# Row normalisation: per-row tensor_scalar instead of a broadcast multiply, and two rows of each tile summed on ScalarE

## The chip, the cores and the metric

The kernel runs on one core of one Trainium2 chip. The metric is the device time of one execution in microseconds (us), as the median of several runs. The profile is of one such execution; its span runs from the first to the last instruction.

## The reference

```python
batch, seq, dim = 32, 512, 1024          # x is float32
sums = np.sum(np.abs(x), axis=-1, keepdims=True)
return (x / (sums + 1e-8)).astype(np.float32)
```

Each of the 16,384 rows of 1024 numbers is divided by the sum of its absolute values. Each element is read once and written once: 67.11 MB in, 67.11 MB out.

## The kernel before

The input is seen as 16,384 rows. A tile holds up to R = 12 rows in each of the 128 partitions, 48 KB per partition and 6.29 MB in all. The list `rows` gives the rows per partition of each of the 11 tiles: ten tiles of 12 rows, and a last one of 8. The function `piece` says which rows of the input belong to a tile: tiles 0, 1 and the last one share one block of 32 rows per partition, and the others have a block of 12 rows per partition each.

Four tile buffers (`BUFS = 4`) rotate. The loop over tiles does four things for each. First, the SP queue issues the load of the whole tile (L78). From the fifth tile on, this issue waits until the store of the tile that had the same buffer has landed. Second, VectorE sums absolute values of all rows of the tile in one `tensor_reduce` (L51), adds the epsilon (L58) and takes the reciprocal (L60), which leaves one factor per row and partition in `inv`. Third, the rows are scaled in place. VectorE multiplies the first `kv` rows in one `tensor_mul` (L61), whose second input is `inv` broadcast along the row, and ScalarE scales the remaining rows one at a time with an activation whose scale is the row's factor (L68). For tile 0, ScalarE takes five rows; for tiles 1 to 6 it takes one; for the last four tiles it takes none. Fourth, the ACT queue, which is ScalarE's own instruction stream, issues the store of the whole tile (L85). The store waits for all scales of the tile, and what stands behind it in ScalarE's stream waits with it.

The order is written by hand (`manual_schedule`), so that each engine runs its instructions in the order of the loop. GpSimd and TensorE do no work on the data.

Of the kernel before, what the change touches and what calls it, by code (L numbers as in the profile page):

```python
# [1 line left out]

# [4 lines left out]

FP32 = mybir.dt.float32
EPS = 1e-8


@with_exitstack
def kernel(
    ctx: ExitStack,
    tc: tile.TileContext,
    x: bass.AP,
    out: bass.AP,
):
    nc = tc.nc
    P = nc.NUM_PARTITIONS  # L20

    x_flat = x.flatten_outer_dims()
    out_flat = out.flatten_outer_dims()
    n, d = x_flat.shape

    R = 12
    BUFS = 4  # L30
    HEAD = 32
    per_partition = n // P
    assert n % P == 0 and (per_partition - HEAD) % R == 0
    rows = [R] * ((per_partition - HEAD) // R + 2) + [HEAD - 2 * R]

    def piece(flat, i):
        head = flat[: P * HEAD, :].rearrange("(p r) d -> p r d", p=P)
        if i < 2:
            return head[:, R * i : R * (i + 1), :]
        if i == len(rows) - 1:  # L40
            return head[:, 2 * R :, :]
        a = P * (HEAD + R * (i - 2))
        return flat[a : a + P * R, :].rearrange("(p r) d -> p r d", p=P)

    sbuf = ctx.enter_context(tc.tile_pool(name="sbuf", bufs=BUFS))
    stats = ctx.enter_context(tc.tile_pool(name="stats", bufs=4))

    def normalize(x_tile, r0, k, kv):

        s = stats.tile([P, R], FP32)  # L50
        nc.vector.tensor_reduce(  # L51
            out=s[:, :k],
            in_=x_tile[:, r0 : r0 + k, :],
            axis=mybir.AxisListType.X,
            op=mybir.AluOpType.add,
            apply_absolute_value=True,
        )
        nc.vector.tensor_scalar_add(out=s[:, :k], in0=s[:, :k], scalar1=EPS)  # L58
        inv = stats.tile([P, R], FP32)
        nc.vector.reciprocal(out=inv[:, :k], in_=s[:, :k])  # L60
        nc.vector.tensor_mul(  # L61
            out=x_tile[:, r0 : r0 + kv, :],
            in0=x_tile[:, r0 : r0 + kv, :],
            in1=inv[:, :kv].unsqueeze(2).to_broadcast([P, kv, d]),
        )
        for r in range(kv, k):
            row = x_tile[:, r0 + r, :]
            nc.scalar.activation(  # L68
                out=row,
                in_=row,  # L70
                func=mybir.ActivationFunctionType.Copy,
                scale=inv[:, r : r + 1],
            )

    with tc.manual_schedule():
        for i, k in enumerate(rows):
            x_tile = sbuf.tile([P, R, d], FP32)
            nc.sync.dma_start(out=x_tile[:, :k, :], in_=piece(x_flat, i))  # L78


            if i == 0:
                normalize(x_tile, 0, k, k - 5)
            else:
                normalize(x_tile, 0, k, k - 1 if i + BUFS < len(rows) else k)
            nc.scalar.dma_start(out=piece(out_flat, i), in_=x_tile[:, :k, :])  # L85


# [1 line left out]
_INS = ['x']  # L89
_OUTS = [((32, 512, 1024), 'float32')]  # L90


# [23 lines left out]
```

## Time and profile before

| what | value |
|---|---|
| median of 11 runs | 316.89 us (316.56 to 320.44) |
| the profiled execution | 316.59 us, of which the span is 315.0 us |
| VectorE (DVE) busy | 268.7 us |
| ScalarE (ACT) busy | 13.5 us |
| L51, sums, 11 instructions | 138.2 us |
| L61, multiplies, 11 instructions | 126.5 us |
| L68, ScalarE's scales, 11 instructions | 12.2 us |
| a 6.29 MB load, from issue to landing, median | 37.9 us |
| a 6.29 MB store, from issue to landing, median | 43.8 us |

In the profile, DVE is VectorE, ACT is ScalarE, and SPq and ACTq are the streams that issue loads and stores. A row of a group of instructions gives the line of the kernel, the engine, the operation, what it writes and reads, how often it ran, its busy time, the mean of one in nanoseconds, and the idle time just before it with what ended that. The line of DMA digits gives, for 40 equal slices of the span, the busy share of the 16 DMA engines in tenths. The rows of the windows give the stretch, its length, the busy time of VectorE, ScalarE and GpSimd with the number of instructions, the clock of TensorE, the DMA share and the GB/s; a DMA packet counts where it ends, so that a share in a short window can pass 1.

### The profile page before, as it was taken

The numbers are of one execution on the slowest core, as the hardware profiler recorded it, in microseconds if no ns is written. First come the engines' busy times: TensorE is split into PE (matmuls) and PEld (weight loads), VectorE is DVE, ScalarE is ACT, GpSimd is POOL, SyncE is SP. The second block draws the span as 40 slices with busy tenths as digits, with TensorE's granted clock in tenths as the row PEclk, the third lists the DMA queues.
The fourth block names the chain that finished last, engine by engine and source line by source line (L and its number), as shares of the span: only waits on it lengthen the run. The fifth ranks groups of instructions, "written<-read, shape, count | busy, mean of one in ns | idle before, by whom it ended". The sixth has DMA issues, their size and how long they took to land.

```text
span 315.0 us, 170 instructions
## 1 busy us (share of the span) xinstructions
DVE 268.7 (85%) x44; ACT 13.5 (4%) x12; POOL 0.2 (0%) x4
## 2 busy tenths in 40 slices
DVE  0079999999999999999995997899699969999910
ACT  0010601001000100100100010000000000000000
POOL 0000000000000000000000000000000000000000
DMA  8999999999999999999999999999999999999997
GB/s 331 468 400 443 456 318 481 400 424 474 400 437 462 400 437 462 400 449 449 400 481 418 400 493 406 400 493 406 400 499 400 406 441 422 470 397 493 400 408 325
DMA packets 3168, 134.22 MB, mean 426 GB/s; under 512 B 352, under 2 KB 352, under 8 KB 352
## 3 DMA queue, kind: packets, MB, share of 16 engines
q1 hardware_dynamic: 1584, 67.11, 49.8%
q10 hardware_dynamic: 1584, 67.11, 49.2%
HBM read 67.11 MB, written 67.11 MB: 426 GB/s over the span
## 4 chain that ended last, share of the span: by engine, by line
DVE 53%; DMA 33%; another core or an unknown queue 9%; issue 0%; SPq 0%; DVEq 0%; ACTq 0%
DVE s L51 27%; DVE x_tile L61 24%; DMA x_tile<-in_x_dram 17%; DMA out_dram<-x_tile 16%; DVE inv L60 1%; DVE s L58 0%; SPq L78 0%; DVEq L60 0%; ACTq L85 0%
## 5 line engine op out<-in xcount | busy, mean ns | idle before, releaser
L51 DVE TENSOR_REDUCE s<-x_tile 128x12 f32<-128x12288 f32 (+1 forms) x11 | 138.2, 12562 | 30.4 <-DMA x_tile<-in_x_dram 30.4
L61 DVE TENSOR_TENSOR x_tile<-x_tile,inv 128x11264 f32<-128x11264 f32 (+3 forms) x11 | 126.5, 11504 | 0.4
L68 ACT ACTIVATE x_tile<-x_tile,inv 128x1024 f32<-128x1024 f32 x11 | 12.2, 1142 | 152.8 <-DVE inv L60 152.8
L60 DVE RECIPROCAL inv<-s 128x12 f32<-128x12 f32 (+1 forms) x11 | 2.5, 225 | 0.9
L58 DVE TENSOR_SCALAR s<-s 128x12 f32<-128x12 f32 (+1 forms) x11 | 1.9, 173 | 0.4
L68 ACT ACT_TABLE_LOAD x1 | 1.3, 1283 | 17.8 <-DMA x_tile<-in_x_dram 17.8
L100 POOL MEMSET const-bfloat16-1.0<- 128x1 bf16 x1 | 0.1, 102 | 0.0
L100 POOL MEMSET const-uint8-127<- 128x1 uint8 x1 | 0.1, 102 | 0.0
L100 POOL MEMSET const-float32-0.0<- 128x1 f32 x1 | 0.1, 98 | 0.2 <-issue 0.2
L100 POOL MEMSET const-float32-1.0<- 128x1 f32 x1 | 0.1, 98 | 0.0
## 6 DMA issues: line engine op xcount, KB each, us to landing
x_tile<-in_x_dram SPq DMA_DIRECT2D x10, 6144.0 KB, 37.9
out_dram<-x_tile ACTq DMA_DIRECT2D x10, 6144.0 KB, 43.8
x_tile<-in_x_dram SPq DMA_DIRECT2D x1, 4096.0 KB, 33.0
out_dram<-x_tile ACTq DMA_DIRECT2D x1, 4096.0 KB, 13.2
```

The lines of the kernel that those rows point to most:

```text
L51: nc.vector.tensor_reduce(out=s[:, :k], in_=x_tile[:, r0 : r0 + k, :], axis=mybir.AxisListType.X, op=mybir.AluOpType.add, apply_absolute_v ...
L58: nc.vector.tensor_scalar_add(out=s[:, :k], in0=s[:, :k], scalar1=EPS)
L60: nc.vector.reciprocal(out=inv[:, :k], in_=s[:, :k])
L61: nc.vector.tensor_mul(out=x_tile[:, r0 : r0 + kv, :], in0=x_tile[:, r0 : r0 + kv, :], in1=inv[:, :kv].unsqueeze(2).to_broadcast([P, kv, d]),)
L68: nc.scalar.activation(out=row, in_=row, func=mybir.ActivationFunctionType.Copy, scale=inv[:, r : r + 1],)
L100: nc = _bacc.Bacc("TRN2", target_bir_lowering=False, num_devices=1)
```

## The change

The scale of a row moves to VectorE for all rows. In place of one `tensor_mul` over many rows it issues one `tensor_scalar_mul` per row, whose factor is a column of `inv`. ScalarE no longer scales. Instead, in each tile but the first, it sums the absolute values of the last `k // 6` rows (two of 12, one of the last tile's 8) with an `Abs` activation, which writes its elements to a scratch tile `junk` in PSUM and its sum to the row's column of `s`. VectorE's `tensor_reduce` covers the other rows. The pool for `s` and `inv` has a buffer count of 11 instead of 4. Loads, stores, tiles, buffers and their order stay as they were.

```diff
-    stats = ctx.enter_context(tc.tile_pool(name="stats", bufs=4))
+    stats = ctx.enter_context(tc.tile_pool(name="stats", bufs=len(rows)))
+    psum = ctx.enter_context(
+        tc.tile_pool(name="psum", bufs=1, space=bass.MemoryType.PSUM)
+    )
+    junk = psum.tile([P, d], FP32)

-    def normalize(x_tile, r0, k, kv):
+    def normalize(x_tile, k, ka):
         s = stats.tile([P, R], FP32)
         nc.vector.tensor_reduce(
-            out=s[:, :k],
-            in_=x_tile[:, r0 : r0 + k, :],
+            out=s[:, : k - ka],
+            in_=x_tile[:, : k - ka, :],
             axis=mybir.AxisListType.X,
             op=mybir.AluOpType.add,
             apply_absolute_value=True,
         )
+        for r in range(k - ka, k):
+            nc.scalar.activation(
+                out=junk[:, :],
+                in_=x_tile[:, r, :],
+                func=mybir.ActivationFunctionType.Abs,
+                accum_out=s[:, r : r + 1],
+            )
         nc.vector.tensor_scalar_add(out=s[:, :k], in0=s[:, :k], scalar1=EPS)
         inv = stats.tile([P, R], FP32)
         nc.vector.reciprocal(out=inv[:, :k], in_=s[:, :k])
-        nc.vector.tensor_mul(
-            out=x_tile[:, r0 : r0 + kv, :],
-            in0=x_tile[:, r0 : r0 + kv, :],
-            in1=inv[:, :kv].unsqueeze(2).to_broadcast([P, kv, d]),
-        )
-        for r in range(kv, k):
-            row = x_tile[:, r0 + r, :]
-            nc.scalar.activation(
-                out=row,
-                in_=row,
-                func=mybir.ActivationFunctionType.Copy,
-                scale=inv[:, r : r + 1],
-            )
+        for r in range(k):
+            row = x_tile[:, r, :]
+            nc.vector.tensor_scalar_mul(out=row, in0=row, scalar1=inv[:, r : r + 1])
...
-            if i == 0:
-                normalize(x_tile, 0, k, k - 5)
-            else:
-                normalize(x_tile, 0, k, k - 1 if i + BUFS < len(rows) else k)
+            normalize(x_tile, k, 0 if i == 0 else k // 6)
```

In the changed kernel the sums are L55 (VectorE) and L63 (ScalarE), the epsilon L69, the reciprocal L71, the row scales L74, the load L79 and the store L81.

## The prediction

> **What bounds the kernel now.** I began with the shares and the 40 slices of the page, because they tell whether an engine or the memory traffic fills the span.
>
> ```profile
> span 315.0 us, 170 instructions
> DVE 268.7 (85%) x44; ACT 13.5 (4%) x12; POOL 0.2 (0%) x4
> ...
> DMA  8999999999999999999999999999999999999997
> ...
> q1 hardware_dynamic: 1584, 67.11, 49.8%
> q10 hardware_dynamic: 1584, 67.11, 49.2%
> HBM read 67.11 MB, written 67.11 MB: 426 GB/s over the span
> ```
>
> VectorE at 85% looks like the bound, but the two queues, q1 (loads) and q10 (stores), hold the 16 DMA engines for 49.8 + 49.2 = 99.0% of the span, 311.9 us. By the windows, the first packets end after 1.5 us and the last ones just before 313.0 us: 311.5 us with no hole in them. The sustained rate is 134.22 MB / 311.5 us = 0.431 MB/us. A 12-row tile is 6.29 MB, so loading and storing it takes 2 x 6.29 / 0.431 = 29.2 us of DMA, while VectorE needs 25.3 us for it. From about 140 us VectorE waits for loads:
>
> ```profile
> DVE s L51 <- DMA x_tile<-in_x_dram: 30.4, 6, 17.7
> ```
>
> Of the 30.4 us, 17.7 are the first load; the other five are later tiles. Then the windows: does the traffic change when VectorE rests?
>
> ```profile
> 165.00:170.00 5.00, 1.42 (x2) 0.00 (x0) 0.00 (x0) 1.00 1.07 462
> 170.00:175.00 5.00, 5.00 (x1) 0.00 (x0) 0.00 (x0) 1.00 1.09 472
> ```
>
> It doesn't: 462 GB/s with VectorE 28% busy, 472 with it always busy (packets count where they end, so a 5 us window scatters around 431). Finally the end, where a chain must surface even under full traffic:
>
> ```profile
> 256.36 12.95 DVE L51 TENSOR_REDUCE s<-x_tile 128x12 f32<-128x12288 f32 x1 [2.52 <-DMA x_tile<-in_x_dram]
> ...
> 269.88 12.96 DVE L61 TENSOR_TENSOR x_tile<-x_tile,inv 128x12288 f32<-128x12288 f32 x1
> 282.76 8.68 DVE L51 TENSOR_REDUCE s<-x_tile 128x8 f32<-128x8192 f32 x1
> ...
> 291.99 8.69 DVE L61 TENSOR_TENSOR x_tile<-x_tile,inv 128x8192 f32<-128x8192 f32 x1
> ```
>
> VectorE ends at 300.7 and the last store (4.19 MB) is issued then and lands 13.2 us later. Its bytes alone take 4.19 / 0.431 = 9.7 us, so up to 313.0 - 9.7 = 303.3 us the DMA engines still drain the store of tile 9. The last store reaches its queue in time, with about 1 us to spare (a first packet ends 0.8 us after its issue at the start). The chain of waits gives VectorE 53% only because it follows this last hand-over backwards; the bound is DMA bytes, from 1.5 to 313.0 us.
>
> **What the Trainium skill says.** "DMA: Bandwidth & Descriptors", section "Queues, rings and completion order": an engine serves its queues round robin, a packet at a time. The trace agrees: from 60 to 250 us, q1 has 50.4% and q10 49.7%. The same page, "Where 436 GB/s comes from", gives a ceiling of 435 GB/s at the SBUF ports; the 434 GB/s of those 190 us sits on it. "SBUF — State Buffer", section "SBUF: two separate sides": computation and DMA have separate ports; the windows above agree. "VectorE: DVE Perf Modes", section "The perf-mode tier table": fp32 tensor_scalar on SBUF runs at two elements a cycle (1227 ns for 2048), tensor_tensor and tensor_reduce at one. The trace agrees on the last two (about 1.054 ns per element); it has no large tensor_scalar.
>
> **The change, part by part.** Fit first: the 7168-element multiply took 7.625 us and the 12288-element reduce 12.950, both 0.155 us plus 1.0417 ns per element.
>
> *Multiply to 12 row scales.* Removed: 11 tensor_tensor, 126.5 us. Added: 128 tensor_scalar of 1024 elements with a pointer scalar. At the skill's two elements a cycle each costs 0.155 + 0.533 = 0.69 us, 88 us in all. At one element a cycle it would be 0.155 + 1.067 = 1.22 us, 156 us in all. The low bound is 0.55 (the fixed part overlapped), the high one 1.31 (1.22 and a pointer fetch of 0.09, which is what "ScalarE: Activation LUTs", section "What ACT_TABLE_LOAD costs", gives for a pointer on ScalarE, an analogy). I take 0.69.
>
> *Two rows' sums to ScalarE.* The nine full tiles after the first reduce 10 rows, 10.82 us instead of 12.95; the last tile 7 rows, 7.62 instead of 8.68. Saved: 9 x 2.13 + 1.06 = 20.2 us of VectorE. ScalarE gets 19 Abs activations. The nearest row is L68, 1.14 us; with an accumulator somewhere between 1.04 and 2.3. Two take 2.1 to 4.6 us beside a 10.82 us reduce.
>
> *ScalarE's old scales* (11 activations, 12.2 us) go. Tile 0 loses a helper: its scale was 7.62 us beside five activations and becomes 12 x 0.69 = 8.3, or 14.7 at one a cycle; its store is issued at about 39.6 (or 45.9) instead of 38.9 us. The cover is the first four loads: 25.2 MB keep the engines fed to 1.5 + 58.4 = 59.9 us without a store. Cost nothing.
>
> *Waits.* VectorE's add at L69 now waits for the activations too; behind it stand the reciprocal and the scales, and behind those the store. On ScalarE's queue, store i waits for VectorE and holds the activations of tile i+1, which start when VectorE starts that tile's reduce. The worst is tile 1: store 0 issued at 39.6, its issue 0.35, table load 1.28, two activations 2.3: done at 43.5, while the reduce runs from 39.5 to 50.3. Cover 6.8 us; nothing is paid. The load of tile i+4 no longer waits for an activation; what comes last there is the store of tile i, as before. Stats buffers go from 4 to 11 and the junk tile sits in PSUM, which nothing else uses: nothing. The number, sizes and order of DMAs on the SP and ACT queues stay the same; POOL has none.
>
> *Sum.* VectorE: 268.7 - 126.5 + 88 - 20.2 = 210 us, 67% of the span. A full tile takes 10.82 + 0.51 + 8.3 = 19.6 us instead of 25.3, against 29.2 us of DMA. The tail: load 9 is gated by the store of tile 5, which advances at the DMA's pace, so it lands at about 256.4 as before, and load 10 at 280.5 (issued 247.5, 33.0 us to landing). VectorE ends tile 9 at 276.0 and tile 10 at 280.5 + 7.62 + 0.51 + 5.5 = 294.1; the last store is issued 6.6 us earlier and simply queues longer. What comes late next is nothing: the bytes are the same. Some 58 us off VectorE, and close to 0 off the span. A small gain is possible: from 295.0 to 313.0 us 7.34 MB moved in 18.0 us, where 0.431 MB/us takes 17.0, so up to 1 us may be lost in a ragged hand-over between the last two stores, which the earlier issue would smooth. I take 0.3.
>
> Against the profiled execution (315.0 span, 1.6 around it, 316.59) this gives 316.3; the median of the 11 runs stands 0.3 higher, at 316.89. Forecast **316.6**.
>
> **Rivals.**
> *A, the row scales are slow and VectorE becomes the bound (slower).* Let p be the price of a row. VectorE without waits: 31.2 (tile 0's scales start) + 8 x 11.33 + 11.33 + 8.13 + 128 p = 141.3 + 128 p; issue and a store that finds an empty queue (9.7 + 2.4 fixed, from load 0's 17.0 us for 14.6 us of bytes) and 1.1 to the span's end add 13.2. So 154.5 + 128 p, which passes 315.0 at p = 1.25 us; below it DMA hides everything, above it each 0.01 us costs 1.3 us. At 1.31 us the span is 322.2, the time 323.8. For it: no row of the page shows the fast mode, and many small instructions replace a long one. Against: the skill's price is 0.69, and even plain one-a-cycle (1.22) stays below the point. Chance 0.07; a further 0.04 for a DMA rate that drops by over 0.5% under VectorE's quicker accesses, about 319, which the windows speak against.
> *B, clearly faster.* For the faster case DMA must move more per us. At 434 GB/s throughout, 134.22 MB take 309.3 us; with 1.5 ahead and 2.0 behind, span 312.8, time 314.4. For it: in the first 60 us only 24.58 MB moved, 1.8 us less than at that rate. Against: that stretch keeps its four loads and its late first store. Chance 0.05.
> *C, the sums or scales don't overlap as said* (activations longer than the reduce): each would need over 5 us, against 1.14 in L68. Below 0.01, in A's share.
>
> **How the numbers follow.** A measurement here can tell about 0.5%, 1.6 us. No change 0.84, faster 0.05, slower 0.11. The likeliest case alone spans 315.8 (the whole ragged us gained) to 317.8 (the upper part of the 11 runs); reaching into A's low end and B's upper end: 315.4 to 318.6.
>
> **What would show it.** Right: DMA queues again near 99% and 426 GB/s; the row scales near 0.69 us; VectorE near 210 us; its waits for loads up from 30 to some 85 us; ScalarE about 23 us plus the table load; the last store issued some 6 us earlier and landing some 6 us later after issue, at the same 314 us. Wrong: a zero in the DMA slices, row scales above 1.25 us, an L69 wait on ScalarE, or DMA at 99% with packets that take longer.

## The result: 319.26 us, some 0.6% slower, and the profile after

The changed kernel takes 319.26 us (median of 13 runs, 318.55 to 320.77) where the kernel before takes 317.01 us (50 runs). The ratio is 1.0064, with a 95% interval of 1.0046 to 1.0081, so the change costs 1.5 to 2.6 us. The forecast was 316.6 us and no change, with a range up to 318.6. The runs of one kernel below, h2, lie in two groups (12 from 316.85 to 318.4 us, 10 from 319.27 to 321.37 us), so that its median of 318.31 stands between them.

The page's shares and groups first. Nearly everything that was said of the engines holds:

```profile
span 317.1 us, 305 instructions
DVE 207.9 (66%) x161; ACT 23.1 (7%) x39; POOL 0.2 (0%) x4
...
DMA  8999999999999999999999999999999999999994
...
q1 hardware_dynamic: 1584, 67.11, 49.5%
q10 hardware_dynamic: 1584, 67.11, 48.9%
q14 instruction: 2, 0.02, 0.0%
...
L55 DVE TENSOR_REDUCE s<-x_tile 128x10 f32<-128x10240 f32 (+2 forms) x11 | 117.9, 10721 | 84.8 <-DMA x_tile<-in_x_dram 84.8
L74 DVE TENSOR_SCALAR x_tile<-x_tile,inv 128x1024 f32<-128x1024 f32 x128 | 85.8, 747 | 0.4
L63 ACT ACTIVATE junk<-x_tile 128x1024 f32<-128x1024 f32 x19 | 19.5, 1027 | 219.6 <-DMA x_tile<-in_x_dram 203.5
```

VectorE's busy time fell to 207.9 us (210 were forecast), its wait for loads rose to 84.8 us (85 were forecast), and L69 never waits for ScalarE. The time that VectorE gave up became waiting, because the DMA engines still hold the bytes. Two things are new. The page lists a third DMA queue, q14, with two packets of 8 KB that it names instruction; below they are called fetches. And the last slice of DMA is a 4 where it was a 7: the end is drawn out.

The end in windows of 1 us (length, busy time of VectorE, ScalarE and GpSimd, clock, DMA share, GB/s), before and then after:

```profile
312.00:313.00 1.00, 0.00 (x0) 0.00 (x0) 0.00 (x0) 1.00 0.83 360
313.00:314.00 1.00, 0.00 (x0) 0.00 (x0) 0.00 (x0) 1.00 0.01 0
314.00:315.00 1.00, 0.00 (x0) 0.00 (x0) 0.00 (x0) 1.00 0.00 0
```

```profile
312.00:313.00 1.00, 0.00 (x0) 0.00 (x0) 0.00 (x0) 1.00 0.84 360
313.00:314.00 1.00, 0.00 (x0) 0.00 (x0) 0.00 (x0) 1.00 0.08 33
314.00:315.00 1.00, 0.00 (x0) 0.00 (x0) 0.00 (x0) 1.00 0.08 33
```

From 312 to 313 us the two are the same. After it, 0.08 of 16 engines' time is about 1.2 us of one engine, and 33 GB/s for 1 us is one packet of 32 KB: in each of these microseconds a single packet of the last store starts. (A window counts a packet where it starts, not where it ends, as the text ahead of the prediction and the prediction have it: this store lands at 316.13 us, and the windows from 315 us on are empty. No step of the argument rests on the difference.) In the changed kernel **one** DMA engine is still working when the other fifteen are done. The trace has the time at which each engine's share of a transfer landed. For the last store, 15 shares landed by 313.79 us before and by 313.97 after; the sixteenth at 313.88 before and at 316.13 after. The last engine was 0.1 us behind and is now 2.2 us behind; the span grew by 2.1 us. (The profiled executions differ by 2.62 us, 319.21 to 316.59: the other 0.5 us lie around the span, and no run here explains them.)

This lag has a history. It is at most 0.2 us until 80 us. The first fetch starts at 96.33 us and takes 0.31 us (1.0% of 16 engines' time in the window from 96 to 98 us):

```profile
q14 instruction: 1, 0.01, 1.0%
```

The load packet behind it takes 2.35 us where 48 KB normally take 1.815. The next landing, at 103 us, shows a lag of 0.86 us, about the sum of the two delays (0.31 + 0.53). At 256 us it is 1.4 us, at 281 us 2.2. Read packet by packet from 46 us on, the trace of before has 0.04 us of delay beyond the usual 1.815 and 1.213 us (48 and 32 KB), that of after 3.2 us, over 19 packets. The trace doesn't name a packet's engine, but the packets of one engine follow each other almost without a gap, so that they can be strung into 16 chains of 88 load and 88 store packets each. The chain that fetched at 96.33 us is the one that ends last, and 2.2 of the 3.2 us, in 10 of the 19 packets, are its own. The second fetch, at 285.22 us, is on another engine and left the lag as it was.

### The profile page after: what moved, and what is told of

The parts are those of the page before. It is cut to its first block, busy times and chain, and to the rows that moved or that the text cites. A ratio compares the mean times of both kernels' runs of the same rounds, so it can differ in the third digit from the quotient of the medians.

```text
span 317.1 us, 305 instructions
## 1 busy us (share of the span) xinstructions
DVE 207.9 (66%) x161; ACT 23.1 (7%) x39; POOL 0.2 (0%) x4
## 4 chain that ended last, share of the span: by engine, by line
another core or an unknown queue 45%; DMA 30%; DVE 17%; SPq 1%; DVEq 0%; issue 0%
DMA x_tile<-in_x_dram 15%; DMA out_dram<-x_tile 14%; DVE s L55 10%; DVE x_tile L74 7%; SPq L79 1%; DVE inv L71 0%; DVEq L107 0%; DVE s L69 0%; DVEq L69 0%
## 5 line engine op out<-in xcount | busy, mean ns | idle before, releaser
L55 DVE TENSOR_REDUCE s<-x_tile 128x10 f32<-128x10240 f32 (+2 forms) x11 | 117.9, 10721 | 84.8 <-DMA x_tile<-in_x_dram 84.8
L74 DVE TENSOR_SCALAR x_tile<-x_tile,inv 128x1024 f32<-128x1024 f32 x128 | 85.8, 747 | 0.4
L63 ACT ACTIVATE junk<-x_tile 128x1024 f32<-128x1024 f32 x19 | 19.5, 1027 | 219.6 <-DMA x_tile<-in_x_dram 203.5
L63 ACT ACT_TABLE_LOAD x1 | 1.3, 1283 | 39.7 <-DVE x_tile L74 39.7
L63 ACT ACTIVATION_READ_ACCUMULATOR junk<-x_tile 128x1 f32 x19 | 3.5, 186 | 0.0
L71 DVE RECIPROCAL inv<-s 128x12 f32<-128x12 f32 (+1 forms) x11 | 2.5, 226 | 0.4
L69 DVE TENSOR_SCALAR s<-s 128x12 f32<-128x12 f32 (+1 forms) x11 | 1.9, 173 | 1.1
```

Of the source, the lines that this page charges most:

```text
L55: nc.vector.tensor_reduce(out=s[:, : k - ka], in_=x_tile[:, : k - ka, :], axis=mybir.AxisListType.X, op=mybir.AluOpType.add, apply_absolut ...
L63: nc.scalar.activation(out=junk[:, :], in_=x_tile[:, r, :], func=mybir.ActivationFunctionType.Abs, accum_out=s[:, r : r + 1],)
L74: nc.vector.tensor_scalar_mul(out=row, in0=row, scalar1=inv[:, r : r + 1])
```

## The experiments

Three questions: which part of the change makes one engine late; does an instruction fetch alone do it; and why do the same fetches cost 2 us in one kernel and little in another? Each ratio is to the kernel before, run again beside it (its medians went from 316.82 to 317.25 us).

**e1, the sums alone.**

```diff
-        for r in range(k):
-            nc.vector.tensor_scalar_mul(out=row, in0=row, scalar1=inv[:, r : r + 1])
+        nc.vector.tensor_mul(out=x_tile[:, :k, :], in0=x_tile[:, :k, :],
+                             in1=inv[:, :k].unsqueeze(2).to_broadcast([P, k, d]))
```

> One part alone: ScalarE sums two rows of each tile but the first, as in the changed kernel, and VectorE scales each tile with one broadcast multiply as the kernel before. VectorE keeps 44 instructions. Theory I (long instruction streams are fetched in 8 KB pieces through one of the 16 DMA engines, which then runs late to the end): no fetch inside the span, the last packets of all 16 engines end within 0.5 us of each other near 313.5 us, time 316.6 to 317.2. Theory II (the row scales on VectorE slow some transfers through the memory ports): also 316.6 to 317.2. Theory III (ScalarE's sums or their scratch tile do it): about 319.2.

Measured: 324.05 us, ratio 1.0217 (1.0189 to 1.0244). All theories missed. The edit also left VectorE alone with tile 0's multiply (12.96 us in place of 7.62), so the first store was issued at 44.21 us. Windows of this kernel:

```profile
60.00:90.00 30.00, 29.82 (x5) 2.30 (x4) 0.00 (x0) 1.00 1.01 398
90.00:120.00 30.00, 29.82 (x6) 4.60 (x8) 0.00 (x0) 1.00 1.01 437
```

From 60 to 90 us the DMA engines are as busy as later (1.01) but move 398 GB/s instead of 437: packets on all engines take longer, and the engines stay busy. f1 below tests whether the late store did it.

**e2, the row scales alone.**

```diff
-            normalize(x_tile, k, 0 if i == 0 else k // 6)
+            normalize(x_tile, k, 0)
```

> The other part alone: VectorE sums all rows and scales them with one tensor_scalar per row, ScalarE only issues stores. VectorE has 161 instructions. Theories I and II: about 319.2, with packets of queue 14 inside the span under theory I. Theory III: 316.6 to 317.2.

Measured: 318.48 us, ratio 1.0049 (1.0029 to 1.0068), one fetch at 80 us, last engine 2.2 us behind, and it is the engine that fetched. ScalarE's sums are not needed for most of the loss, so theory III falls.

**e3, the kernel before with 132 small memsets on idle GpSimd.**

```diff
...
+            for _ in range(12):
+                nc.gpsimd.memset(pad[:, :], 0.0)
             x_tile = sbuf.tile([P, R, d], FP32)
```

> The kernel before with 132 memsets of one number per partition added on GpSimd, which nothing else waits for. VectorE and ScalarE are as before. Theory I, if any engine's instruction stream is fetched that way: a queue 14 packet early in the span (GpSimd runs its memsets in the first 20 us), one engine late by 0.8 us or more to the end, time 317.5 to 319.3. Theory I, if only VectorE's long stream counts, and theories II and III: 316.6 to 317.2.

Measured: 320.35 us, ratio 1.0101 (1.0083 to 1.0119), a fetch at 11.7 us, last engine 3.1 us behind, again the one that fetched. No instruction of VectorE or ScalarE was changed, and no data moved. Here instructions on an idle engine, which nobody waits for, cost 1%.

**e4, e1 with 117 small memsets on VectorE.**

```diff
...
+            for _ in range(k - 1):
+                nc.vector.memset(pad[:, :], 0.0)
             nc.scalar.dma_start(out=piece(out_flat, i), in_=x_tile[:, :k, :])
```

> The kernel of the sums alone, with k - 1 memsets of one number per partition added on VectorE after each tile's multiply (117 in all), so that VectorE has 161 instructions as in the changed kernel but no row scale. Theory I: queue 14 packets at about 100 and 285 us, one engine late by some 2 us at the end, about 319.2. Theories II and III (II: no row scales, so no harm): 316.6 to 317.2 for II, 319.2 for III only if the sums alone give it as well.

Measured: 324.1 us, ratio 1.0221 (1.0202 to 1.0241), as e1 and outside all ranges: with its first store at 44.12 us, what the fetches add can't be told from what the late store costs. Repeated as f2.

**f1, the sums alone, tile 0 as before.** Edit: in e1, `kv = k - 5` for tile 0, whose other five rows ScalarE scales.

> The sums on ScalarE alone again, but with tile 0 scaled as in the kernel before (seven rows on VectorE beside five on ScalarE), so that the first store is issued at 38.9 us and not at 44. Theory I (8 KB instruction fetches set one DMA engine back): the streams are short, a fetch comes after 285 us at the earliest, time 316.8 to 317.8. If ScalarE's sums themselves cost the time seen in e1_sums_only: 322 to 324. If the late first store did: back to 317.

Measured: 317.36 us, ratio 1.0002 (0.9981 to 1.0022). Its first store is issued at 38.80 us, and between 60 and 90 us it moves

```profile
60.00:90.00 30.00, 29.82 (x6) 4.54 (x8) 0.00 (x0) 1.00 1.01 437
```

So the sums cost nothing that can be told from noise, and a first store that is 5.4 us later cost e1 6.7 us, with slower packets on all engines. Why those packets are slow was not settled. The fetches came at 260.6 and 292.8 us, the first of them earlier than expected.

**f2, f1 with 117 memsets on VectorE.**

```diff
...
+            for c in range(R * i, R * i + k - 1):
+                nc.vector.memset(pad[:, c : c + 1], 0.0)
             nc.scalar.dma_start(out=piece(out_flat, i), in_=x_tile[:, :k, :])
```

> The kernel of f1_sums_tile0 with 117 memsets of one number per partition added on VectorE (k - 1 after each tile's multiply, each to its own column, without waits): VectorE has 161 instructions as in the changed kernel, but no row scale. Theory I: queue 14 packets near 100 and 285 us, the last landing about 2 us behind that of the other engines, 1.5 to 2.5 us over f1_sums_tile0. Theory II (the row scales' own memory accesses do it): the same as f1_sums_tile0 within 0.5 us.

Measured: 317.61 us, ratio 1.0014 (0.9998 to 1.0030). The fetches came at 105.4 us, with VectorE's added instructions, and at 261.6, where f1 has one too. The first delayed its engine by 0.31 + 0.54 us, as in the changed kernel. But at the end the last engine was 0.5 us behind, not 2. The fetch is there and the loss is not. By the ranges set down, this speaks for theory II, which g1 below tests; if theory I is to stand, something must make the lag grow in the changed kernel and not here.

**f3, the pad of e3 late** (a copy that depends on tile 9's reciprocal, then 131 memsets on GpSimd).

> The kernel before with a copy of one number and 131 memsets on GpSimd that begin when tile 9's reciprocal is done (about 270 us), where e3_pool_pad had its 132 at the start. If a fetch costs what it takes from its engine once: one 0.3 to 0.8 us delay whenever it comes, and e3's 3.5 us came from something else in its early fetch. If the delay grows from tile to tile once one engine is out of step: late is cheap, 317.0 to 317.9; at e3's 320.3 if only the number of instructions counts.

Measured: 317.21 us, ratio 0.9999 (0.9978 to 1.0019), fetch at 295.0 us, last engine 0.2 us behind. The number of instructions alone costs nothing that can be told from noise.

**f4, 44 memsets in place of e3's 132.**

> e3_pool_pad with four memsets per tile in place of twelve, 44 in all, so that GpSimd's stream ends before the point at which e3's was fetched (after 78 of its recorded instructions). If the fetch is the cause: no queue 14 packet inside the span, 316.6 to 317.2. If GpSimd's instructions cost by their number: a third of e3's 3.5 us, about 318.0.

Measured: 317.64 us, ratio 1.0010 (0.9988 to 1.0032), no fetch inside the span, last engine 0.3 us behind. The median lies above the first range and below the second. The interval holds no change, and excludes e3's 1% and just excludes the third of it (0.37%).

Comparing the traces gave a second half for theory I. Each DMA engine alternates between a load packet and a store packet. In the kernel before, whose first store is issued at 38.91 us, the engines take their first store packet at two times: 4 of 16 at 43.4 to 43.9 us, the other 12 one packet later, at 45.3 to 45.9. From there on they work in **two groups**, half a cycle of one load and one store packet apart. In the changed kernel the first store comes 0.34 us later, no engine catches the earlier place, and all 16 alternate **in one step** (45.3 to 45.7 us). From the timelines, before and after:

```profile
38.91 0.38 ACTq L85 DMA_DIRECT2D out_dram<-x_tile  x1
```

```profile
39.25 0.37 ACTq L81 DMA_DIRECT2D out_dram<-x_tile  x1
```

The 0.34 us come from tile 0: twelve row scales on VectorE (8.04 us) in place of seven rows there (7.62) beside five on ScalarE.

**g1, the changed kernel with tile 0 as before.**

```diff
+        if ka == 0:
+            kv = 0
+            nc.vector.tensor_mul(...)          # rows 0 to 6
+            for r in range(k - 5, k): nc.scalar.activation(...)
+        for r in range(kv):
```

> The changed kernel with tile 0 alone scaled as in the kernel before (seven rows on VectorE beside five on ScalarE); tiles 1 to 10 keep their row scales and ScalarE's sums. The first store is issued at about 38.9 us instead of 39.25. Theory I with its second half (a fetch costs 0.3 to 0.9 us where the engines alternate between load and store packets in two groups, as behind a first store at 38.9 us, and grows to 2 us or more where 15 of them keep one step, as behind one at 39.3): 317.2 to 318.0. Theory II (the row scales' own accesses do it): 319.2, as the changed kernel.

Measured: 317.32 us, ratio 1.0023 (1.0003 to 1.0042). First store at 38.93 us, fetches at 127.1 and 261.9 us, last engine 0.2 us behind. 116 row scales are left and the loss is nearly gone, so theory II falls.

**g2, g3 and g4** were to set step and fetch one by one on the kernel before (their expectations follow in this order): g2 with a memset of 230 numbers on VectorE ahead of tile 0's multiply, g3 with that and a GpSimd pad from tile 2 on, g4 with the pad alone.

> The kernel before with one memset of 230 numbers per partition (0.4 us) on VectorE between the reciprocal and the multiply of tile 0, so that the first store is issued at about 39.3 us as in the changed kernel; no other instruction is added, and no instruction fetch falls inside the span. If the time of the first store alone costs: 318.5 to 319.5. If it needs a fetch as well: 316.7 to 317.4, with all engines ending together.

> g2_store0_later with a copy of one number and 131 memsets on GpSimd that begin at tile 2's reciprocal (about 78 us), so that one 8 KB fetch falls near 100 us, about where the changed kernel had its first. Theory I with its second half: one engine late by some 2 us at the end, 318.3 to 319.5. If the fetch costs the same whatever the step of the engines: as g4_fetch_only.

> The same GpSimd instructions as in g3_later_and_fetch on the kernel before, without the memset in tile 0: first store at 38.9 us, one fetch near 100 us. Theory I with its second half: one engine late by 0.5 to 0.9 us, 317.2 to 318.0. If the step of the engines doesn't matter: as g3_later_and_fetch.

Measured: g2 317.0 us (ratio 0.9983, 0.9960 to 1.0007), g3 317.27 (1.0014, 0.9987 to 1.0041), g4 317.38 (1.0007, 0.9991 to 1.0023). The memset overlapped with its neighbours and moved nothing: the first store of g2 and g3 was issued at 38.89 us and their engines ran in two groups. So all three are of the two-group kind, and they show that a fetch near 100 us (g3, g4) costs at most 0.41% there, the upper end of the wider interval. The other half needed a longer memset.

**h1, g2 with 500 numbers.**

> The kernel before with a memset of 500 numbers per partition on VectorE ahead of tile 0's multiply (230 moved the first store by nothing in g2_store0_later, since the memset overlapped). The first store should now be issued at 39.2 to 39.4 us, as in the changed kernel. No fetch inside the span. Theory I with its second half (in-step engines alone cost nothing, a fetch is needed): 316.7 to 317.4, with the first store packets of all 16 engines between 45.4 and 46.1 us. Rival (a first store at 39.3 costs by itself): 318.5 to 319.5.

Measured: 317.67 us, ratio 1.0036 (1.0005 to 1.0067). The time lies between the two ranges, and the interval just excludes no change. First store at 39.16 us, all 16 engines in one step, no fetch inside the span, and in the profiled execution (316.95 us) all land together (15th 313.86, last 313.88). Its runs spread, though: nine up to 318.05, five from 319.21 to 321.0. What those five lost isn't in the trace, so it isn't excluded that one step costs time without a fetch in some executions.

**h2, h1 with the fetch.**

> h1_store0_39_3 with g3's copy and 131 memsets on GpSimd from tile 2's reciprocal on: one fetch near 100 us. Theory I with its second half: the engine that fetches falls back from tile to tile, last landing 1.5 to 3 us behind, 318.3 to 320. Rival (a fetch costs its 0.3 to 0.9 us whatever the step): 317.0 to 317.8.

Measured: median 318.31 us, ratio 1.0045 (1.0016 to 1.0073), the two groups of runs named above. The profiled one took 319.29 us: first store at 39.34 us, one step, fetch at 101.5 us, and the last engine falls from 0.5 us behind at 139 us to 1.1 at 256 and 2.2 at the end. Its last windows repeat those of the changed kernel:

```profile
313.00:314.00 1.00, 0.00 (x0) 0.00 (x0) 0.00 (x0) 1.00 0.08 33
314.00:315.00 1.00, 0.00 (x0) 0.00 (x0) 0.00 (x0) 1.00 0.08 33
```

The median just reaches theory I's range, but the trace speaks against the theory. The engine that fetched lost 0.31 + 0.21 us and ended with the others. The engine that ended 2.2 us late fetched nothing inside the span: its first store packet began at 46.0 us, 0.4 us after the last of the other fifteen, it was 0.6 us behind at 52 us, and ten slow packets, 2.2 us in all, followed from 82 us on. So an engine that is late for another reason falls back in the same way; the fetch is one way to make it late, and not a necessary one. Nor do the times tell h1 and h2 apart: 5 of 14 runs lie above 319.2 us without the fetch, 10 of 22 with it, and the two intervals nearly coincide.

**h3, the changed kernel with one row of tile 0 on ScalarE.**

```diff
-        for r in range(k):
+        kv = k - 1 if ka == 0 else k
+        for r in range(kv):
...
+        for r in range(kv, k):
+            nc.scalar.activation(out=row, in_=row, func=..., scale=inv[:, r : r + 1])
```

> The changed kernel with one row of tile 0 scaled on ScalarE beside VectorE's eleven, so that the first store is issued some 0.6 us earlier, near 38.6 us; the other 127 row scales and ScalarE's sums stay. Theory I with its second half: the engines split into two groups and the fetches cost little, 317.0 to 318.0. Rival (the number of instructions, or the row scales of tiles 1 to 10): 318.8 to 319.4.

Measured: 317.70 us (317.27 to 318.24), ratio 1.0019 (1.0001 to 1.0038). One row of 128 moved; 127 row scales, 19 sums and both fetches (98.2 and 281.9 us) stayed. No run reaches the changed kernel's lowest, 318.55 us. From its timeline and its last windows:

```profile
38.77 0.37 ACTq L90 DMA_DIRECT2D out_dram<-x_tile  x1
```

```profile
313.00:314.00 1.00, 0.00 (x0) 0.00 (x0) 0.00 (x0) 1.00 0.01 0
314.00:315.00 1.00, 0.00 (x0) 0.00 (x0) 0.00 (x0) 1.00 0.00 0
```

The tail is gone. The engine that fetched at 98.2 us lost 0.31 + 0.54 us, as in the changed kernel, and had no further slow packet. (h3 also brings ScalarE's table load forward, from 39.7 to 17.9 us. That isn't the cause: e2 has no activation at all and shows the lag all the same.) All traces but those of e1 and e4, whose first store comes at 44 us:

| kernel | first store issued, us | engines in the early place | fetch before 130 us | last engine behind the 15th, us | last landing, us |
|---|---|---|---|---|---|
| before, g2, f4, f3, f1 | 38.80 to 38.91 | 4 to 14 | none | 0.1 to 0.3 | 313.9 to 314.8 |
| f2, g1, g3, g4, h3 | 38.74 to 38.93 | 6 to 10 | one | 0.1 to 0.5 | 313.9 to 314.6 |
| h1 | 39.16 | 0 | none | 0.0 | 313.9 |
| changed, e2 | 39.25, 39.30 | 0 | one, on the last engine | 2.2 | 316.1, 315.9 |
| h2 | 39.34 | 0 | one, on another engine | 2.2 | 316.2 |
| e3 | 39.30 | 1 | one, at 11.7, on the last engine | 3.1 | 316.8 |

All four kernels that leave an engine over 2 us late have their engines in one step (15 of 16 in e3), and none of the ten with two groups does, although five of these have an early fetch. So the step, which the time of the first store sets, divides them. In one step an engine that is late falls further back: in the changed kernel, e2 and e3 it is the one that fetched (in e3 also the one engine in the early place), in h2 it isn't. One step without a late engine costs nothing in h1's profiled execution. Each row rests on one profiled execution per kernel. (In e3 the fetch did both: it delayed its engine's part of load 0 by 0.4 us, and with it the first store.)

## Why the prediction was wrong, point by point

**The bound: right.** DMA holds the span in both kernels, and 15 of 16 engines are done by 314.0 us (313.8 before).

**The engines: right.** Of the row scale, 0.69 us was taken; one measured 747 ns in its row, and twelve followed each other in 8.04 us, 0.67 each. The price in "VectorE: DVE Perf Modes" of the Trainium skill, section "The perf-mode tier table" (two elements a cycle), holds. VectorE's 207.9 us, its 84.8 us of waiting and the last store's issue at 294.7 us (294.1 from the sum) came as worked out. Rival A did not occur: 0.67 is far from 1.25.

**"Tile 0 ... Cost nothing": wrong, and this is the step that failed.** The cover named was bytes: four loads that keep the engines fed to 59.9 us. It was true of bytes, but the time of the first store also sets how the engines' packets interleave. At 0.34 us later the engines run in one step, in which a lag of 0.86 us grew to 2.2. With one row of tile 0 moved back to ScalarE (h3) the lag at the end was 0.2 us and the time 317.70 us in place of 319.26. At 5.4 us later, in e1 against f1, packets on all engines were slow between 46 and 90 us.

**"The number, sizes and order of DMAs ... stay the same ... nothing": true of the two queues that it names, and incomplete.** It counted the DMAs that the kernel issues. Two more came with the longer instruction streams: 8 KB each, 0.02 MB in all, and the first took 0.31 us of one engine and 0.53 us from its next packet. That is where the changed kernel's lag begins. No other engine took over packets of the late one: it moved its 88 loads and 88 stores like the rest. But the fetch alone isn't the loss: in f2, g1 and h3 it delayed its engine by the same 0.84 us or so, and at the end the last engine was 0.2 to 0.5 us behind.

**"What comes late next is nothing: the bytes are the same": wrong** for the same reasons. What came late was the end of one engine's sixteenth of the bytes.

**The ragged last microsecond** that was to give 0.3 us gave nothing: the 15 engines were not done earlier than before.

**The 0.04 set aside** for a DMA rate that drops had named about 319 us. That it came so close is luck: some packets were slower, but not by VectorE's accesses, since g1 and h3 keep nearly all of them. A fetch term alone (0.84 us, 317.4 in all) would still have missed; the growth to 2.2 us could be read from no row of the profile before. Why a late engine falls further back in one step stays open.

## What to carry to other kernels

When the DMA engines are full from end to end, ask what else will use them: here 8 KB packets of the queue named instruction ran on them too, so that over 100 instructions more on VectorE or on idle GpSimd could put one DMA engine late (changed, e2, e3), and the slowest of 16 sets the end. There, look at the spread of the last transfer's landings and not at the mean DMA share, which stayed at 98.4% here. Do not call a shift of the first store free because bytes cover it; moving one row of tile 0 back to ScalarE (h3) gave most of the loss back, and neither that nor g1 beat the kernel before. And ask of a trace that shows the expected lag which engine is late: h2 had the expected lag on an engine that the explanation didn't name.

## What the runs showed of the hardware

- The profile shows 8 KB instruction packets on q14. VectorE's stream brought them (e2), GpSimd's (e3), and by the look of it ScalarE's (f1, where only that stream is longer and the fetches come at 260.6 and 292.8 us). A fetch before 130 us appeared in each kernel that gave one engine over 100 more instructions early on, and none with 44 more (f4).
- A 48 KB packet takes 1.815 us on its engine, load or store, with VectorE busy or not; in the kernel before only two packets after 46 us exceeded that by over 0.015 us. Slow packets are thus visible one by one. They come without a fetch too: f4, which has none inside the span, shows 23, with 5.7 us of delay in all, spread over the engines, and its last landing is 1.0 us later.
- With all engines in one step, an engine that was 0.5 to 0.9 us late got slower packets again and again (0.86 us at 103 us, 2.2 at 281 us in the changed kernel; likewise e2 and h2). In two groups, the engine that had fetched early got no further slow packet in f2, g1 and h3; in g4 it got six more, 0.5 us in all, and still didn't end late. Why one step punishes a late engine is not explained by these runs.
- Two kernels that differ in when the first store is issued (38.80 and 44.21 us) differ by 6.7 us, with DMA busy throughout. What slows the packets in that case stays open.
